# Latent and sparse prompt attention: outputs by query, divided by the softmax sum behind the value product

## The chip, the cores and the metric

The kernel runs on one core of one Trainium2 chip. The metric is the device time of one execution in microseconds. The median of three runs of the kernel before is 2569.67 us, the lowest 2569.64 and the highest 2575.63.

## What is computed

One step of a two-layer encoder for 512 prompt frames of a new stream and 64 sample frames of an old one with 1024 cached positions. Each layer runs a feed-forward block, then one projection whose columns feed four kinds of attention, then an output projection, then a second feed-forward block. The two kinds that the change touches end in the same softmax; cut to its core:

```python
def _softmax_attend(q, k, v, mask):                     # latent attention (MLA), 4 heads, value width 64
    s = jnp.einsum('bqhd,bkhd->bhqk', q, k).astype(jnp.float32) * (q.shape[-1] ** -0.5)
    p = jax.nn.softmax(jnp.where(mask[None, None], s, NEG_INF), axis=-1).astype(v.dtype)
    return jnp.einsum('bhqk,bkhd->bqhd', p, v)

def block(qp, qb, qib, wib):                            # sparse attention (DSA), 4 heads, one value of width 64
    ...
    _, idx = lax.top_k(score, n_sel)
    ...
    s = jnp.einsum('bqhd,bqkd->bhqk', qb, ks).astype(jnp.float32) * (DH_B ** -0.5)
    p = jax.nn.softmax(jnp.where(valid[:, None], s, NEG_INF), axis=-1).astype(vs.dtype)
    return jnp.einsum('bhqk,bqkd->bhqd', p, vs)
```

The other two kinds are stick-breaking attention and differential attention. Prompt queries are taken in four tiles of 128 (tile tt sees 128(tt+1) keys), the 64 sample queries form a fifth.

## The kernel before

A layer's mixing stage has two parts. In the first the projection's columns are computed piece by piece (matmuls of L629 to L631 into psG, a long supply of work for TensorE that depends on little), and beside them run MLA, the stick-breaking tiles, the top-k of the sparse attention's sample scores and of its prompt scores. In the second the differential and the sparse tiles run, with the rest of the prompt top-k, beside the output projection (L1095). The parts are generators that are merged by weights; the order of each engine's instructions is then fixed by a list scheduler when the program is built, from the order in which the code issues the work and from the buffers that it finds free. No wait or order is written by hand.

A prompt tile of MLA (L1157 to L1177) and of DSA (L1460 to L1485) handles two heads j at a time. `softmax_pair` (L698) puts the scores of each head into a psA bank, takes the negative row maximum on VectorE (L709), the exponential on ScalarE with the row sum (L710), and the reciprocals of both sums on VectorE (L712, tile rs). VectorE then multiplies each head's exponentials by its reciprocal (L1171 for MLA, L1479 for DSA). `pT_prompt` (L715) turns them with one transpose on TensorE for each block of 128 keys (L101) and copies the turned blocks out of psT, head 0 on VectorE (L87), head 1 on ScalarE (L85). `av_prompt` (L726, matmul in L730) multiplies with the values: the value block (128 keys x 64) is the stationary operand, the turned weights (128 x 128) are the moving one, head 0 fills rows 0 to 63 of the psO bank and head 1 rows 64 to 127. What stands in psO is the output by feature, which `put_o` copies into the operand of the output projection. Both kinds have 8 such calls in a layer, so there are 32 in the program. The stick-breaking and differential tiles use `pT_prompt` and `av_prompt` too, and they and the sample tiles use the same psO bank, of which there is one; psA, psT and psG have two banks each, psQ one.

Other lines that are named below: `scaled` (L97) is a ScalarE activation with a scale per row; a stick-breaking tile's weights are made by `stick_weights` with L1311, L1314, L1317 and L1318 on VectorE and L1312, L1313 and L1319 (the last step) on ScalarE; the prompt top-k repeats L977 (MAX) and L978 (MATCH_REPLACE) on VectorE 16 times for each of three query tiles; L1328 and L579 on VectorE rotate and split keys and queries; L1002 swaps rows on TensorE for the sample top-k; L1364 (VectorE) combines the two softmaxes of a differential tile, L760 is the exponential of a sample tile.

Of the kernel before, what the change touches and what calls it, by code (L numbers as in the profile page):

```python
# [13 lines left out]
ALU = mybir.AluOpType  # L14
# [22 lines left out]
class Builder:  # L37
# [17 lines left out]
    def t(self, pool, shape, dt=F32, tag="t"):  # L55
        return pool.tile(shape, dt, tag=tag, name=self.name(tag))
# [658 lines left out]
    def pT_prompt(self, P, i, k):  # L715

        ps = self.psT()
        for b in range(i + 1):
            self.transpose(ps[:, b * 128:b * 128 + 128], P[:, b * 128:b * 128 + 128])
        t = self.t(self.mp, [128, 512], tag="PT")  # L720
        n = (i + 1) * 128
# [3 lines left out]
    def av_prompt(self, PTs, V, i):  # L725
# [5 lines left out]
                                      start=(kt == 0), stop=(kt == i))  # L731
        return ps

    def put_o(self, o, c, t0, m, src, p0=0, p1=128):
        self.evac(self.turn(c), o[0][p0:p1, c, t0:t0 + m], src)

# [44 lines left out]

    def av_sample(self, out, PT, Vc, Vn):

        for j in range(8):
            self.nc.tensor.matmul(out, Vc(j), PT[:, j, :], start=(j == 0), stop=False)  # L785
        self.nc.tensor.matmul(out, Vn, PT[0:64, 8, :], start=False, stop=True)

# [96 lines left out]
    def ix_b(self, wi, kip, kis):  # L884
# [7 lines left out]
        for hb in range(2):  # L892
            for tt, m, ps, r in self.win(800 + 256 * hb, 256, tts=range(1, 5)):
# [3 lines left out]
                if tt < 4:  # L897
                    L = 128 * (tt + 1)
                    for j in range(4):
                        h = hb * 4 + j  # L900
                        pa = self.psA()
                        for k in range(2):
                            nc.tensor.matmul(pa[:, 0:L], qT[:, j * 128:j * 128 + 128], kip[:, k * 512:k * 512 + L],
                                             start=(k == 0), stop=(k == 1))
                        rl = t([128, 512], tag="PT")
                        nc.scalar.activation(rl[:, 0:L], pa[:, 0:L], AF.Relu)
# [196 lines left out]
    def mla(self, o):  # L1103
        nc, I, l = self.nc, self.i, self.l
# [3 lines left out]
        kT0, kT1, vp, lat = self.four(self.xp, "xT")  # L1108
# [43 lines left out]
        for tt, (t0, m) in enumerate(TT):  # L1152
            q = t([128, 4, 96], tag="q")
            nc.sync.dma_start(q[:m].rearrange("p h d -> p (h d)"), self.dq["a"][t0:t0 + m, :])
            ps = self.psQ()
            for h in range(4):
                self.transpose(ps[:96, h * m:h * m + m], q[:m, h, :])  # L1157
            qT = t([128, 512], tag="qT")
            self.scaled(qT[:96, 0:4 * m], ps[:96, 0:4 * m], scale)
            yield  # L1160
            if tt < 4:
                L = t0 + 128
                for pr in range(2):
                    def scores(j, out):
                        h = 2 * pr + j
                        nc.tensor.matmul(out, qT[:96, h * 128:h * 128 + 128], kT[pr][:96, j * 512:j * 512 + L],
                                         start=True, stop=True)
                    P, rs = self.softmax_pair(scores, L)
                    PT = []
                    for j in range(2):  # L1170
                        nc.vector.tensor_scalar(P[:, j, 0:L], P[:, j, 0:L], rs[:, j:j + 1], None, ALU.mult)  # L1171
                        PT.append(self.pT_prompt(P[:, j, :], tt, j))
                    po = self.av_prompt(PT, lambda kt, j: vp[:, kt * 256 + (2 * pr + j) * 64:
                                                             kt * 256 + (2 * pr + j) * 64 + 64], tt)
                    self.put_o(o, pr, t0, 128, po[:, 0:128])
                    yield
            else:  # L1177
                ps = self.psQ()
                for h in range(4):
                    nc.tensor.matmul(ps[:, h * 64:h * 64 + 64], wkT[:, h * 128:h * 128 + 128],  # L1180
                                     qT[0:64, h * 64:h * 64 + 64], start=True, stop=True)
                ql = t([128, 256], tag="ql")
                nc.scalar.copy(ql, ps[:, 0:256])
                ol = t([128, 256], tag="ql")
                for pr in range(2):
                    lq, lr = ql[:, pr * 128:pr * 128 + 128], qT[64:96, pr * 128:pr * 128 + 128]

                    def mms(out, s):
                        nc.tensor.matmul(out, lq, lats[:, s], start=True, stop=False)
                        nc.tensor.matmul(out, lr, krs[64:96, s], start=False, stop=True)  # L1190
                    P, rs = self.softmax_sample(self.sample_scores(mms))
                    nc.vector.tensor_scalar(P[:, 0:LS], P[:, 0:LS], rs, None, ALU.mult)
                    PT = self.pT_sample(P)
                    pol = self.psO()
                    self.av_sample(pol[:, 0:128], PT, lambda j: cr[j], mrow[4][0:64, 0:128])
                    nc.scalar.copy(ol[:, pr * 128:pr * 128 + 128], pol[:, 0:128])
                    yield
                po = self.psO()
                for h in range(4):
                    nc.tensor.matmul(po[64 * (h % 2):64 * (h % 2) + 64, (h // 2) * 64:(h // 2) * 64 + 64],  # L1200
                                     wkv[:, 1, h * 64:h * 64 + 64], ol[:, h * 64:h * 64 + 64], start=True, stop=True)
                for pr in range(2):
                    self.put_o(o, pr, 512, 64, po[:, pr * 64:pr * 64 + 64])
# [236 lines left out]
    def dsa(self, o, sel):  # L1440
        nc, I, O, l = self.nc, self.i, self.o, self.l
# [8 lines left out]
        kv = t([128, 4, 128], tag="kv")  # L1450
# [7 lines left out]
        for tt, (t0, m) in ((tt, TT[tt]) for tt in DSA_ORDER):  # L1458
# [3 lines left out]
            if tt < 4:  # L1462
                L = t0 + 128
# [5 lines left out]
                for pr in range(2):  # L1469
                    def scores(j, out):  # L1470
                        lhs = qT[:, (2 * pr + j) * 128:(2 * pr + j) * 128 + 128]
                        nc.tensor.matmul(out, lhs, kp[:, 0:L], start=True, stop=False)  # L1472
                        nc.tensor.matmul(out, lhs, kp[:, 512:512 + L], start=False, stop=(tt == 0))
                        if tt:
                            nc.tensor.matmul(out, self.identR, bias, start=False, stop=True)
                    P, rs = self.softmax_pair(scores, L, tt == 0, True)
                    PT = []
                    for j in range(2):
                        nc.vector.tensor_scalar(P[:, j, 0:L], P[:, j, 0:L], rs[:, j:j + 1], None, ALU.mult)  # L1479
                        PT.append(self.pT_prompt(P[:, j, :], tt, j))  # L1480
                    po = self.av_prompt(PT, lambda kt, j: kv[:, kt, 64:128], tt)
                    self.put_o(o, pr, t0, 128, po[:, 0:128])
                    yield
            else:
# [3 lines left out]
                for pr in range(2):  # L1488
# [12 lines left out]
                    P, rs = self.softmax_sample(self.sample_scores(mms), True)  # L1501
                    nc.vector.tensor_scalar(P[:, 0:LS], P[:, 0:LS], rs, None, ALU.mult)
                    PT = self.pT_sample(P, True)
                    po = self.psO()
# [32 lines left out]
    def run(self):  # L1537
        self.load_x()
        for l in range(DEPTH):
# [13 lines left out]
DSA_ORDER = (4, 0, 1, 2, 3)  # L1553
STICK_AT = (0, 1)
BUFS = dict(Pb=4, op=6, P=4, mrow=5, gq=4, gx=3, rt=3, qs=3, qT=2, PT=3, q=2, qm=1, mx=8, sm=6, rs=6, m1=3, s1=4, lr=4,
            ki=1, ql=2, m8=4)

_INS = ['x_prompt', 'x_sample', 'cache_mla', 'cache_dsa', 'cache_sb', 'cache_diff', 'norm_ff1', 'norm_mix', 'w_in',
        'mla_q_norm', 'mla_w_qb', 'mla_kv_norm', 'mla_w_kvb', 'diff_lambda', 'diff_norm', 'w_out', 'norm_ff2',
# [60 lines left out]
```

## Time and profile before

| | |
|---|---|
| median of the runs | 2569.67 us |
| the profiled execution | 2569.89 us |
| its span | 2568.1 us |
| TensorE (PE) busy | 2459.5 us, 96% |
| VectorE (DVE) busy | 1878.8 us, 73% |
| ScalarE (ACT) busy | 1251.2 us, 49% |

The span is the time from the first to the last instruction of the profiled execution; 1.8 us lie around it. In the trace the mixing stage of layer 0 lies at about 425 to 870 us and that of layer 1 at about 1690 to 2130 us; the rest is feed-forward. MLA's prompt tiles run between 565 and 620 and between 1815 and 1871 us, the stick-breaking prompt tiles up to 715 and 1982 us, DSA's prompt tiles at 770 to 870 and 2040 to 2127 us. A float32 matmul is two instructions in the trace, so L730 shows 640 instructions for its 320 matmuls. In the timeline a matmul's time overlaps the next one's; the distance between two starts is what it costs TensorE.

### The profile page before, as it was taken

How to read it: one execution, taken by the hardware profiler on the slowest of the kernel's cores; microseconds unless marked ns; L12 is line 12 of the kernel's file. 1: busy time of each engine (PE TensorE's matmuls, PEld its weight loads, DVE VectorE, ACT ScalarE, POOL GpSimd, SP SyncE). 2: the span in 40 equal slices, each digit the busy share in tenths (PEclk: the TensorE clock that was granted, in tenths of full speed). 3: DMA queues.
4: the chain of work that ended last, by engine and by line, in shares of the span. 5: the costliest groups of instructions: out<-in, count | busy, mean ns of one | idle time of the engine just before them, and what ended most of it. 6: DMA issues, size and time to landing. Idle time of an engine off the chain costs nothing. (4 is left out here: it accounts for less than half of the span.)

```text
span 2568.1 us, 44800 instructions
## 1 busy us (share of the span) xinstructions
PE 2459.5 (96%) x17275; PEld 2262.5 (88%) x17275; DVE 1878.8 (73%) x3866; ACT 1251.2 (49%) x2684; POOL 144.4 (6%) x255
## 2 busy tenths in 40 slices
PE   8999998999998899999999999989999988999998
PEld 7999998887775699999989999978877667999997
DVE  7858574798976696766697675648999676958574
ACT  5525253544555553544554353535445564625352
POOL 0000002200100100000100000022001001000001
PEclk9999998999999999999999999989999999999999
DMA  4313223243331123231423232233342312322222
GB/s 136 117 65 105 77 91 96 75 126 89 83 124 46 67 90 107 84 107 58 120 86 125 74 110 71 73 106 90 114 105 70 106 49 75 114 70 97 99 67 70
DMA packets 188581, 233.40 MB, mean 91 GB/s; under 512 B 79452, under 2 KB 143120, under 8 KB 188368
## 3 DMA queue, kind: packets, MB, share of 16 engines
q1 hardware_dynamic: 188368, 230.54, 28.9%
q8 instruction: 136, 2.23, 0.4%
q14 instruction: 77, 0.63, 0.1%
HBM read 211.76 MB, written 18.73 MB: 90 GB/s over the span
## 5 line engine op out<-in xcount | busy, mean ns | idle before, releaser
L563 PE MATMUL psA<-h,opd 128*128 128x288 f32 x3936 | 526.8, 296 | 0.0
L563 PEld LDWEIGHTS psA<-h,opd 128*128 128x128 f32 x3936 | 525.4, 189 | 0.0
L439 PE MATMUL psA<-T,opd 128*128 128x288 f32 x2880 | 396.2, 295 | 0.0
L439 PEld LDWEIGHTS psA<-T,opd 128*128 128x128 f32 x2880 | 387.2, 188 | 0.1
L439 PE MATMUL psA<-aH,opd 128*128 128x288 f32 x2240 | 366.6, 300 | 14.0 <-ACT aH L389 11.8
L439 PEld LDWEIGHTS psA<-aH,opd 128*128 128x128 f32 x2240 | 324.5, 191 | 17.0 <-ACT aH L389 14.2
L425 ACT CAST opd<-S 128x512 fp32r<-128x512 f32 x320 | 194.5, 621 | 160.6 <-PE psA L563 124.2
L426 DVE TENSOR_TENSOR opd<-S,opd 128x512 fp32r<-128x512 f32 x320 | 215.1, 688 | 75.9 <-ACT opd L425 72.4
L425 ACT CAST opd<-raw 128x512 fp32r<-128x512 f32 x272 | 163.8, 620 | 167.6 <-PE psA L563 82.2
L426 DVE TENSOR_TENSOR opd<-raw,opd 128x512 fp32r<-128x512 f32 x272 | 181.5, 687 | 66.1 <-ACT opd L425 66.0
L629 PE MATMUL psG<-whl,aH 128*128 128x256 f32 (+1 forms) x672 | 202.5, 302 | 15.7 <-ACT whl L299 15.3
L630 PE MATMUL psG<-whl,aH 128*128 128x256 f32 (+1 forms) x672 | 200.4, 298 | 0.8 <-DVE whl L300 0.7
L439 PE MATMUL psA<-aL,opd 128*128 128x288 f32 x1120 | 198.3, 300 | 0.0
L631 PE MATMUL psG<-whl,aL 128*128 128x256 f32 (+1 forms) x672 | 196.8, 293 | 0.0
L559 DVE TENSOR_TENSOR opd<-raw,opd 128x512 fp32r<-128x512 f32 (+1 forms) x176 | 114.1, 653 | 90.1 <-ACT opd L558 88.4
L558 ACT CAST opd<-raw 128x512 fp32r<-128x512 f32 (+1 forms) x176 | 103.5, 592 | 156.0 <-PE psA L563 120.4
L507 ACT COPY e<-psA 128x288 f32<-128x288 f32 x240 | 96.1, 400 | 159.8 <-PE psA L439 159.1
L568 DVE SCALAR_TENSOR_TENSOR xT<-psA,xT 128x288 f32<-128x288 f32 x192 | 79.5, 452 | 123.9 <-PE psA L563 123.6
L439 PEld LDWEIGHTS psA<-aL,opd 128*128 128x128 f32 x1120 | 168.4, 192 | 0.2
L1095 PE MATMUL psG<-op,whl 128*128 128x288 f32 x512 | 145.8, 412 | 2.2 <-DVE op L1397 1.0
L629 PEld LDWEIGHTS psG<-whl,aH 128*128 128x128 f32 x672 | 128.3, 191 | 20.7 <-ACT whl L299 15.7
L630 PEld LDWEIGHTS psG<-whl,aH 128*128 128x128 f32 x672 | 128.3, 191 | 8.3 <-issue 3.3
(428 smaller groups left out, 4073.2 us busy)
## 6 DMA issues: line engine op xcount, KB each, us to landing
raw<-in_wgu SPq DMA_DIRECT2D x176, 512.0 KB, 3.7
raw<-in_wdn SPq DMA_DIRECT2D x128, 256.0 KB, 3.0
raw<-in_w_in SPq DMA_DIRECT2D x36, 512.0 KB, 3.8
whl<-in_w_out SPq DMA_DIRECT2D x48, 256.0 KB, 3.9
raw<-in_wdn SPq DMA_DIRECT2D x48, 192.0 KB, 2.6
xs<-xT SPq DMA_DIRECT2D x16, 288.0 KB, 2.1
xT<-xs SPq DMA_DIRECT2D x8, 576.0 KB, 5.2
g<-in_wdn SPq DMA_DIRECT2D x16, 192.0 KB, 2.5
```

The source lines that it names most:

```text
L425: self.nc.scalar.copy(o[:, 0, :], x)
L426: self.nc.vector.tensor_tensor(o[:, 1, :], x, o[:, 0, :], ALU.subtract)
L439: self.nc.tensor.matmul(ps, o[:, w, c * 128:c * 128 + 128], a[:, c, :], start=start and i + c == 0, stop=stop and i == 2 and c == 3, skip_ ...
L507: nc.scalar.copy(t, ps)
L558: nc.scalar.copy(o[:, 0, 0:n * 128], r)
L559: nc.vector.tensor_tensor(o[:, 1, 0:n * 128], r, o[:, 0, 0:n * 128], ALU.subtract)
L563: nc.tensor.matmul(ps[h][:, 0:HALF], o[:, a, c * 128:c * 128 + 128], H[j][c][:, b, h * HALF:h * HALF + HALF], start=j + i + c == 0, stop=j ...
L568: nc.vector.scalar_tensor_tensor(xv, ps[h][:, 0:HALF], 0.5, xv, ALU.mult, ALU.add)
L629: nc.tensor.matmul(ps[:m, 0:n], a, hi, start=(c == 0), stop=False)
L630: nc.tensor.matmul(ps[:m, 0:n], a, lo, start=False, stop=False)
L631: nc.tensor.matmul(ps[:m, 0:n], b, hi, start=False, stop=(c == KC - 1))
L1095: nc.tensor.matmul(ps[k][:, 0:HALF], wt[:, sl], a[:, hs[k]], start=(c == 0), stop=(c == n - 1))
```

## The change

In the MLA and DSA prompt tiles the two multiplications by rs on VectorE are gone: the exponentials are turned as they are. A new function takes the place of `av_prompt` there. It makes the turned block (128 keys x 128 queries) the stationary operand and the value block (128 x 64) the moving one, so that a head's output comes by query, 128 rows of 64 columns, head 0 in columns 0 to 63 of the psO bank and head 1 in columns 64 to 127, one head after the other. Two ScalarE activations copy them to a new SBUF tile ot and multiply each row by its reciprocal. One transpose on TensorE turns ot into columns 128 to 255 of the same psO bank, and `put_o` copies it from there as before. The stick-breaking, differential and sample tiles are as they were.

```diff
+    def av_rows(self, PTs, V, i, rs):
+
+        ps = self.psO()
+        ot = self.t(self.mp, [128, 128], tag="ot")
+        for j in range(2):
+            out = ps[:, 64 * j:64 * j + 64]
+            for kt in range(i + 1):
+                self.nc.tensor.matmul(out, PTs[j][:, kt * 128:kt * 128 + 128], V(kt, j), start=(kt == 0), stop=(kt == i))
+        for j in range(2):
+            self.scaled(ot[:, 64 * j:64 * j + 64], ps[:, 64 * j:64 * j + 64], rs[:, j:j + 1])
+        self.transpose(ps[:, 128:256], ot)
+        return ps[:, 128:256]
...
                     P, rs = self.softmax_pair(scores, L)
-                    PT = []
-                    for j in range(2):
-                        nc.vector.tensor_scalar(P[:, j, 0:L], P[:, j, 0:L], rs[:, j:j + 1], None, ALU.mult)
-                        PT.append(self.pT_prompt(P[:, j, :], tt, j))
-                    po = self.av_prompt(PT, lambda kt, j: vp[:, kt * 256 + (2 * pr + j) * 64:
-                                                             kt * 256 + (2 * pr + j) * 64 + 64], tt)
+                    PT = [self.pT_prompt(P[:, j, :], tt, j) for j in range(2)]
+                    po = self.av_rows(PT, lambda kt, j: vp[:, kt * 256 + (2 * pr + j) * 64:
+                                                           kt * 256 + (2 * pr + j) * 64 + 64], tt, rs)
...
                     P, rs = self.softmax_pair(scores, L, tt == 0, True)
-                    PT = []
-                    for j in range(2):
-                        nc.vector.tensor_scalar(P[:, j, 0:L], P[:, j, 0:L], rs[:, j:j + 1], None, ALU.mult)
-                        PT.append(self.pT_prompt(P[:, j, :], tt, j))
-                    po = self.av_prompt(PT, lambda kt, j: kv[:, kt, 64:128], tt)
+                    PT = [self.pT_prompt(P[:, j, :], tt, j) for j in range(2)]
+                    po = self.av_rows(PT, lambda kt, j: kv[:, kt, 64:128], tt, rs)
...
-            ki=1, ql=2, m8=4)
+            ki=1, ql=2, m8=4, ot=2)
```

The new lines push the later ones down: in the changed kernel the new matmul is L741, L1166 is L1179, L1189 is L1199, L1311 is L1321, L1419 is L1429, L1095 is L1108, L977 and L978 are L990 and L991. The schedule changes with the new durations and buffers, all through the mixing stages.

On TensorE, an MLA tile with two key blocks in layer 0 (tt 1, the first pair of heads). A row is line, operation, output and inputs, and the size of the output; x2 stands for two alike in a row. Before:

```order
L629 MATMUL psG_7403<-whl_7398,aH_4315 128x256
L630 MATMUL psG_7403<-whl_7399,aH_4315 128x256
L631 MATMUL psG_7403<-whl_7398,aL_4316 128x256
L730 MATMUL psO_6577<-PT_6569,xT_6097 64x128
L730 MATMUL psO_6577<-PT_6575,xT_6097 64x128
L730 MATMUL psO_6577<-PT_6569,xT_6097 64x128
L730 MATMUL psO_6577<-PT_6575,xT_6097 64x128
L1166 MATMUL psA_6628<-xT_6097,qT_6624 128x384
```

After:

```order
L1179 MATMUL psA_6597<-xT_6097,qT_6551 128x256
L741 MATMUL psO_6579<-xT_6097,PT_6572 128x64 x2
L741 MATMUL psO_6579<-xT_6097,PT_6577 128x64 x2
L101 MATMUL psQ_6716<-ident,q_6714 96x128 x4
L630 MATMUL psG_7419<-whl_7415,aH_4315 128x256
L631 MATMUL psG_7419<-whl_7414,aL_4316 128x256
L101 MATMUL psO_6579<-ident,ot_6580 128x128
L629 MATMUL psG_7419<-whl_7414,aH_4315 128x256
```

The four matmuls that took the two heads by turns are now two of one head and two of the other, and six other matmuls stand between the last of them and the new transpose of ot, which needs ScalarE's two copies.

On TensorE, the first DSA tile of layer 0 (one key block). Before:

```order
L101 MATMUL psT_8752<-ident,Pb_8728 128x128
L730 MATMUL psO_8756<-PT_8749,kv_8272 64x128
L1419 MATMUL psA_8824<-aH_8161,qT_8795 128x256
L1095 MATMUL psG_9428<-op_6951,whl_9184 128x288
L730 MATMUL psO_8756<-PT_8754,kv_8272 64x128
L1419 MATMUL psA_8830<-aH_8161,qT_8795 128x256
```

After:

```order
L101 MATMUL psT_8766<-ident,Pb_8744 128x128
L741 MATMUL psO_8770<-kv_8288,PT_8764 128x64
L1429 MATMUL psA_8823<-aH_8177,qT_8813 128x256
L101 MATMUL psQ_9026<-ident,qs_9023 128x128 x2
L741 MATMUL psO_8770<-kv_8288,PT_8768 128x64
L1108 MATMUL psG_9454<-op_6107,whl_9208 128x288
L1108 MATMUL psG_9453<-op_6967,whl_9208 128x288
L101 MATMUL psO_8770<-ident,ot_8771 128x128
```

Here only two matmuls of the output projection stand between the last value product and the new transpose.

On VectorE, in layer 0, in a stick-breaking tile with three key blocks (L1311, in the changed kernel L1321, begins its weights P; S is the score tile of the prompt top-k). Before:

```order
L978 MATCH_REPLACE S_719_5149<-m_1674_9181,S_719_5149 128x512
L1311 TENSOR_SCALAR P_7215<-P_7214 128x2x384
L977 MAX m_1702_9269<-S_719_5149 128x8
L300 TENSOR_TENSOR whl_7947<-raw_7945,whl_7946 128x1024
L978 MATCH_REPLACE S_719_5149<-m_1702_9269,S_719_5149 128x512
L1314 TENSOR_TENSOR P_7215<-P_7214,P_7215 128x2x384
```

After:

```order
L991 MATCH_REPLACE S_719_5149<-m_1716_9299,S_719_5149 128x512
L1321 TENSOR_SCALAR P_7231<-P_7230 128x2x384
L990 MAX m_1717_9302<-S_719_5149 128x8
L991 MATCH_REPLACE S_719_5149<-m_1717_9302,S_719_5149 128x512
L990 MAX m_1761_9441<-S_719_5149 128x8
L991 MATCH_REPLACE S_719_5149<-m_1761_9441,S_719_5149 128x512
L1324 TENSOR_TENSOR P_7231<-P_7230,P_7231 128x2x384
```

One more step of the prompt top-k stands there, and the split of a weight (L300) has gone behind. Up to the last stick-breaking weights of a layer, VectorE's list holds three to four more MAX and three to four more MATCH_REPLACE of 128x512 than before.

## Rows read from the trace of the kernel before

**Rows 1.** The page: busy time by engine; the chain that ended last, by engine.

```profile
PE 2459.5 (96%) x17275; PEld 2262.5 (88%) x17275; DVE 1878.8 (73%) x3866; ACT 1251.2 (49%) x2684; POOL 144.4 (6%) x255
PE 21%; DVE 2%; ACT 1%; DMA 0%; issue 0%; SPq 0%; ACTq 0%; DVEq 0%
```

**Rows 2.** Busy time by stretch: stick-breaking of layer 1, DSA of both layers.

```profile
core 0: us, PE busy (x) PEld busy (x) DVE busy (x) ACT busy (x) POOL busy (x), PEclk, DMA share, GB/s
740.00:870.00 130.00, 120.63 (x680) 85.03 (x680) 92.31 (x282) 78.42 (x228) 4.99 (x6) 0.96 0.17 51
...
1910.00:1980.00 70.00, 63.13 (x434) 50.82 (x433) 67.76 (x117) 37.70 (x68) 9.07 (x14) 0.95 0.26 72
2010.00:2126.00 116.00, 107.06 (x627) 74.67 (x627) 84.55 (x265) 73.56 (x215) 3.37 (x4) 0.99 0.16 47
```

**Rows 3.** TensorE's timeline: start, time, line, operands; value products of one and three blocks.

```profile
566.60 0.28 PE L631 MATMUL psG<-whl,aL 128*128 128x256 f32 x1
566.71 0.28 PE L629 MATMUL psG<-whl,aH 128*128 128x256 f32 x1
566.93 0.44 PE L730 MATMUL psO<-PT,xT 128*64 128x128 f32 x4
567.29 0.39 PE L630 MATMUL psG<-whl,aH 128*128 128x256 f32 x1
...
598.14 0.88 PE L730 MATMUL psO<-PT,xT 128*64 128x128 f32 x12
598.95 0.39 PE L630 MATMUL psG<-whl,aH 128*128 128x256 f32 x1
```

**Rows 4.** Timelines of weight loads (one moving column each) and of TensorE (transposes).

```profile
423.78 0.52 PEld L287 LDWEIGHTS psQ<-ones,ssum 128*128 128x128 f32 x4 [1.75 <-DVE ssum L281]
...
2060.28 1.09 PE L101 MATMUL psT<-ident,P 128*128 128x128 f32 x8
2061.13 0.42 PE L1419 MATMUL psA<-aH,qT 128*128 128x384 f32 x1
```

**Rows 5.** VectorE's busy time in L1171 alone, then in L1479 alone, layer 0.

```profile
550.00:620.00 70.00, 5.50 (x16) 1.00 0.32 87
...
740.00:870.00 130.00, 5.41 (x16) 0.96 0.17 51
```

**Rows 6.** ScalarE groups of 128x64 in L97: busy, mean ns, idle before.

```profile
L97 ACT ACTIVATE gq<-psG,rtok 128x64 f32<-128x64 f32 x8 | 2.4, 311 | 5.0 <-DMA xT<-xs 4.4 <-DVE rt L579 0.5
...
L97 ACT ACTIVATE P<-psT 128x64 f32<-128x64 f32 x4 | 0.9, 224 | 0.4 <-PE psT L1270 0.4
```

**Rows 7.** ScalarE's timeline: the copy behind the value product at 598.14.

```profile
599.06 0.27 ACT L85 COPY op<-psO 128x128 f32<-128x128 f32 x1
```

**Rows 8.** TensorE's timeline: transposes of the last two stick-breaking tiles, layers 0 and 1.

```profile
704.92 1.97 PE L101 MATMUL psT<-ident,P 128*128 128x128 f32 x8 [3.00 <-ACT P L1319]
...
713.75 1.03 PE L101 MATMUL psT<-ident,P 128*128 128x128 f32 x8
...
1972.29 1.97 PE L101 MATMUL psT<-ident,P 128*128 128x128 f32 x8 [4.26 <-ACT P L1319]
...
1979.34 0.93 PE L101 MATMUL psT<-ident,P 128*128 128x128 f32 x7
```

**Rows 9.** ScalarE's timeline: the last step of the last stick-breaking tile, both layers.

```profile
712.22 1.06 ACT L1319 ACTIVATE P<-P 128x1024 f32<-128x1024 f32 x1 [2.22 <-DVE P L1318]
...
1978.16 1.07 ACT L1319 ACTIVATE P<-P 128x1024 f32<-128x1024 f32 x1
```

**Rows 10.** VectorE groups of the prompt top-k, 512 columns: busy, mean ns, idle.

```profile
L977 DVE MAX8 m<-S 128x8 f32<-128x512 f32 x32 | 21.9, 685 | 0.3
...
L978 DVE MATCH_REPLACE8 S<-m,S 128x512 f32<-128x512 f32 x32 | 21.6, 675 | 0.0
```

**Rows 11.** TensorE's waits at 740 to 870; the chain of waits at 2060.

```profile
PE psT L101 <- DVE P L1364: 3.0, 2, 1.9
...
2060.41 0.54 DVE Pb L1479 x2
```

## The prediction

> **What bounds the kernel now.** I read the busy times first, then the chain that ended last, then the busy time by stretch, and then the waits of the stretches in which changed lines run. TensorE is busy 96% of the span, VectorE 73%, and the chain that ended last is mostly TensorE [rows 1]: what lengthens TensorE's list lengthens the kernel, except where TensorE waits. It waits in two of the stretches. In the stick-breaking part of layer 1 (1910 to 1980) VectorE is busy 67.76 of 70 us and TensorE 63.13 [rows 2]: VectorE sets the end there. The last two tiles show it. In layer 0 TensorE idles 3.00 us for ScalarE's L1319, the last step of a tile's weights, and in layer 1 4.26 us; the eight transposes behind take 1.97 us against 1.03 at 713.75 [rows 8], so another 1 us is lost to the clock that fell in the wait. The last tile of each layer starts directly behind its own L1319, which ends at 712.22 + 1.06 = 713.28 and at 1978.16 + 1.07 = 1979.23 [rows 9], with the transposes at 713.75 and 1979.34 [rows 8]. In the DSA stretches TensorE idles 9 of 130 and 9 of 116 us, VectorE is at 71 and 73%, ScalarE at 60 and 63% [rows 2]: no engine is full, and the waits are for the chain of a softmax through all three.
>
> **TensorE's work.** Before, a value product of one key block runs from 566.93 to 567.29, one of three blocks from 598.14 to 598.95 [rows 3]: 0.81 - 0.36 = 0.45 for two blocks, so 0.22 a block (both heads side by side) and 0.14 over. It also starts 0.22 behind its predecessor where the row ahead has 0.11 [rows 3], 0.10 late. A layer has 8 calls with 20 blocks for each kind: 20 x 0.22 + 8 x 0.24 = 6.3 us. In DSA two calls a layer are cut in two by other matmuls, as in the order shown; each cut pays 0.36 + 0.10 once more, less its block: I take 7.2 us.
>
> After, a block is two instructions for each head, and each loads 128 columns of weights for only 64 moving ones. The row nearest to that is the group whose four loads serve one moving column each: four in 0.52 us, so at most 0.13 each; transposes with 128 moving columns go eight in 2061.13 - 2060.28 = 0.85, 0.106 each [rows 4]. With 1 and with 128 columns the step is the same, so the load sets it, and for 64 columns I take 0.11: 4 x 0.11 = 0.44 a block, 8.8 us for 20, and 8 transposes of ot at 0.106, 0.85. That is 9.65 us a layer and kind: 3.35 more in MLA, 2.45 more in DSA, **11.6 us over both layers**. The other end: were the step set by the moving columns, 0.106 x 64/128 = 0.053, a block would cost 0.21, the kind 4.2 + 0.85 = 5.1, and TensorE would save 1.2 and 2.1 a layer.
>
> **VectorE and ScalarE.** VectorE loses 16 instructions a layer in each kind, 5.50 and 5.41 us busy [rows 5], 21.8 us in all. No TensorE wait stands on L1171, so in MLA they were covered by the projection's matmuls. In DSA 0.54 us of L1479 stands on the chain once [rows 11]. ScalarE gains 64 copies of 128x64: 311 ns is the row with a scale per row, 224 the one without [rows 6]. I take 0.3, 0.61 a pair, 19.5 us in all (14.3 by the lower row). ScalarE has room for them, but they queue behind its exponentials.
>
> **The turn-around of ot.** A copy behind a value product now starts 599.06 - 598.95 = 0.11 after the next matmul [rows 3, 7]. The transpose of ot waits for the pair on ScalarE: some 0.2 from the last value product's start to its result, 0.61 for the pair, 0.1 and 0.1 to hand over, 1.0 us. What covers it is what the order puts between. In the MLA tile shown those are four transposes and two projection matmuls, 6 x 0.11 = 0.66: 0.3 short. Through the rest of MLA the order has six or more, mostly; I count 0.8 us a layer. In the DSA tile shown there are only two matmuls, and one later DSA tile has a single one; summed over the eight calls I come to 1.3 us a layer, if ScalarE takes the pair at once, none if the stall falls into a wait that is there anyway. The last DSA tile has its turn-around at the end of the layer's mixing, 0.5 us.
>
> **Where it lands: MLA and stick-breaking.** TensorE gets 3.35 + 0.8 = 4.15 us more per layer ahead of the last stick-breaking tiles, and has 4.0 us (3.00 and 1.0 of slow clock) to recover in layer 0, some 5.3 in layer 1 [rows 8]. But recovering takes that VectorE comes earlier, and the order fills most of its 5.4 us: three or four more MAX and MATCH_REPLACE at 685 and 675 ns, 5.0 us [rows 10], stand ahead of the last weights, for a few small splits and rotations that go behind, of which some filled gaps only. I take 1.5 us earlier for the last L1319 in each layer (0.3 to 2.6). Layer 0: the last transposes then start at 713.28 - 1.5 + 0.1 = 711.9, 1.8 earlier than before. TensorE is there in time: 713.75 - 4.0 + 4.15 = 713.9, less 35 projection matmuls (0.11 to 0.12 each, 4.1) and L1002 (0.4) that the new order leaves for behind, 709.4. These are still to be done: -1.8 + 4.5 = **+2.7**. Layer 1: 13 matmuls go behind, 1.5 us; TensorE would be there at 1979.34 - 5.3 + 4.15 - 1.5 = 1976.7, VectorE lets it go at 1977.8: -1.5 + 1.5 = **0**. Behind that both layers are TensorE's, and the rest of VectorE's saving (the top-k that is done early) buys nothing.
>
> **Where it lands: DSA.** TensorE +2.45, stalls 0.9 of the 1.3, the end 0.5; less 0.8 for L1479 on the chain (it is there 0.54 once, and some tiles wait less visibly), and less 0.6 because a part of the added 3.9 falls into the 7% and 8% in which TensorE idles and VectorE, relieved, hands over L1364 (3.0 us of waits [rows 11]) a little sooner: **+2.45 a layer**, between 0 and 4.3.
>
> **Sum.** 2.7 + 0 + 2 x 2.45 = +7.6 on the profiled 2569.89; that run is 0.2 over the median. I put it at **2577 us**, with 2570 to 2584 for this case by its terms' bounds. A measurement here can tell about 0.3%, 7.7 us, so the forecast lies at the edge of what can be told from no change.
>
> A page speaks to this too. The Trainium skill, "TensorEngine Tiling (Array Packing)", Key Properties, says that a change of tiling mode drains TensorE. The 0.10 and 0.14 us at the ends of a group with 64 output rows agree with that; with 128 rows they go, which the sum already has from the rows.
>
> **Rivals.**
> (a) *Nothing is given back.* TensorE's 11.6, the stalls of 2 x (0.8 + 1.3) and the ends 2 x 0.5 all lie on its path, and the waits for L1319 stay as they are because the top-k in front takes up VectorE's time: +16.8, 2586.5. For it: the order does put 5.0 us of top-k there. Against: 3 to 4 us of idle TensorE lie directly behind. It decides for slower from the point where more than half of the 16.8 stays. 0.13.
> (b) *ScalarE holds the single psO bank.* The pair and the transpose keep psO some 1.3 us longer, and L1319 or an exponential of 1.06 us [rows 9] ahead of the pair adds to it; the differential and sample tiles queue for the same bank. Half of 1.06 at each of 16 DSA tiles is +8.5, with the case's own +7.6 some 2585. For it: ScalarE's 60% in DSA [rows 2]; against: most uses of psO lie further apart. 0.07.
> (c) *VectorE was the bound.* Its saving comes off the chain: the waits of 4.0 and 5.3 us vanish (+0.2 and -1.2), and DSA, whose chain loses 5.4 us of VectorE's 92, gets 2.5 a layer back: -6, 2564, beyond the edge of faster if DSA gives 3.5. For it: VectorE at 97% in the stretch 1910 to 1980 [rows 2]. Against: the order refills it, and in DSA it is at 71%. 0.14, of which 0.08 faster.
> (d) *The moving columns set the step.* TensorE saves 2 x (1.2 + 2.1) = 6.6; with the waits that VectorE gives back (1.5 a layer) and half of the stalls, 2.1, it is -7.5, 2562. Against: the one-column group that takes as long as 128 columns [rows 4]. 0.05.
> The Trainium skill has this rule in "TensorE: Matmul & The Clock Gate", Back-to-back issue gap, for an isolated matmul: the gap goes with the number of moving columns. The trace disagrees by the group just named.
>
> **How the numbers follow.** The forecast's case has 0.61, of which 0.40 lies within 0.3% and 0.21 above. With (a) 0.13 and (b) 0.07 slower, (c) 0.08 faster and 0.06 within, (d) 0.05 faster: faster 0.13, same 0.46, slower 0.41. The range goes from (c), 2564, to 2588, just over (a) and (b); it leaves out the faster half of (c) with (d) and what goes wrong in more than one way.
>
> **What would show it.** Right: L741 steps of 0.11; the wait for the last stick-breaking tiles shorter by some 1.5 us a layer and moved to the very last tile; stretches 740 to 870 and 2010 to 2126 longer by 2 to 3 us; the transposes of ot waiting for L97 under 2 us a layer. Wrong: steps of 0.05, or waits of ot of 1 us at every tile, or DSA stretches that end sooner than before.

## The result

The changed kernel takes 2588.51 us in the median of five runs (2582.75 to 2594.87), beside 2571.12 us for the kernel before in the same five rounds (2569.64 to 2575.63). The ratio is 1.0063 with a 95% interval of 1.0047 to 1.0078: 0.63% slower, 16 us. The forecast was 2577 us, 7.3 us more than before. The profiled execution of the changed kernel took 2590.39 us, 20.5 us more than that of before, so its stretches add up to a little more than the medians differ.

The page of the changed kernel, busy time by engine, answers to [rows 1]:

```profile
PE 2473.9 (96%) x17307; PEld 2290.6 (88%) x17307; DVE 1860.8 (72%) x3802; ACT 1263.5 (49%) x2748; POOL 146.6 (6%) x255
```

VectorE is 18 us less busy, ScalarE 12 us more, TensorE 14 us more. Of the 20.5 us by which this execution is longer, 14 are TensorE's busy time, and the other 6 are time in which TensorE idles.

Where the time went is seen in the stretch from the first latent score to the last output-projection matmul of a layer. The first two rows are before, the other two after; the columns are the stretch, its length, the busy time of TensorE, its weight loads, VectorE, ScalarE and GpSimd, then TensorE's granted clock as a share of 2.4 GHz, and the DMA's share and rate. (MLA of layer 1 begins at 1826.70 us before, not at 1815.)

```profile
561.11:882.70 321.59, 305.43 (x1909) 229.83 (x1909) 257.77 (x653) 175.29 (x464) 25.93 (x42) 0.98 0.30 86
1826.70:2148.77 322.07, 304.42 (x1910) 228.83 (x1909) 257.03 (x654) 174.96 (x463) 26.09 (x42) 0.98 0.30 86
```

```profile
561.72:889.03 327.31, 307.96 (x1926) 238.85 (x1926) 248.20 (x621) 181.27 (x497) 27.41 (x42) 0.99 0.29 84
1834.62:2169.26 334.64, 315.25 (x1926) 247.21 (x1926) 249.06 (x622) 181.97 (x496) 26.44 (x42) 0.95 0.29 83
```

Layer 0 takes 5.7 us more, layer 1 takes 12.6 us more, though both have the same instructions, in orders that differ in places. Layer 1 also ran at a mean clock of 0.95 where before had 0.98, layer 0 at 0.99. Some 2 us more lie outside the two stretches, 0.6 ahead of the first and 1.6 between them.

The new value products, from TensorE's timeline of the changed kernel (start, time, line, operands):

```profile
598.10 0.78 PE L741 MATMUL psO<-xT,PT 128*128 128x64 f32 x6
598.72 0.39 PE L101 MATMUL psQ<-ident,kc 128*128 128x128 f32 x2
...
603.11 1.00 PE L741 MATMUL psO<-xT,PT 128*128 128x64 f32 x8
603.92 0.37 PE L631 MATMUL psG<-whl,aL 128*128 128x256 f32 x1
```

Six steps take 0.62 us, eight take 0.81: 0.10 each, for 64 moving columns. That is the step of [rows 4], where 128 columns of weights are loaded for one or for 128 moving columns; the moving columns do not set it. A block costs 0.41 us against 0.22 in [rows 3].

The transposes of ot and ScalarE's pairs, from the changed kernel's view of the tile ot:

```profile
L97 ACT ACTIVATE ot<-psO,rs x64: 304/308/317, 566.8 to 2148.6; 128x64 f32<-128x64 f32 x64
...
  PEld psO L101: 2.4, 7
...
  PE psO L101: 0.5, 2
```

A copy takes 308 ns in the median. In the whole program TensorE's matmuls waited for ot twice, 0.5 us together, and its weight loads, which run ahead of them, seven times, 2.4 us; so TensorE lost between 0.5 and some 3 us to it.

TensorE's waits in the latent and stick-breaking parts of the changed kernel, layer 0 and then layer 1 (us in total, times, the longest); the last two lines are the waits for L1319 before, in the same parts of both layers, and L1329 is what was L1319:

```profile
PE psG L629 <- DVE gx L623: 2.7, 1, 2.7
PE psT L101 <- ACT P L1329: 2.4, 2, 1.3
PE psG L629 <- DVE rt L579: 1.1, 1, 1.1
```

```profile
PE psT L101 <- ACT P L1329: 6.2, 3, 3.4
PE psG L629 <- DVE rt L579: 0.6, 1, 0.6
```

```profile
PE psT L101 <- ACT P L1319: 3.9, 2, 3.0
...
PE psT L101 <- ACT P L1319: 5.3, 2, 4.3
```

And where they stand in the timeline, beside [rows 8]: layer 0, then layer 1.

```profile
705.07 0.39 PE L629 MATMUL psG<-whl,aH 128*128 128x256 f32 x1 [2.72 <-DVE gx L623]
713.02 1.09 PE L101 MATMUL psT<-ident,P 128*128 128x128 f32 x8 [1.11 <-ACT P L1329]
...
1981.65 1.09 PE L101 MATMUL psT<-ident,P 128*128 128x128 f32 x8 [2.00 <-ACT P L1329]
1987.98 1.97 PE L101 MATMUL psT<-ident,P 128*128 128x128 f32 x8 [3.42 <-ACT P L1329]
```

Of the last two tiles of a layer, TensorE waited before at one, the last but one, 3.00 and 4.26 us. After, it waits twice: in layer 1 at both tiles, in layer 0 at the last one and, ahead of the last but one, under another name. There TensorE's next projection matmul needs a psG bank that VectorE's L623 has yet to read. L623 could have read it from 701.31 on, when ScalarE's L622 had ended, but it stands behind steps of the stick-breaking weights in VectorE's list:

```profile
700.64 2.33 DVE L1327 TENSOR_TENSOR_SCAN P<-zero,P 128x512 f32<-128x512 f32 x2
...
703.48 1.22 DVE L1328 TENSOR_TENSOR P<-P,P 128x1024 f32<-128x1024 f32 x1
704.61 0.41 DVE L623 TENSOR_TENSOR gx<-gx,psG 64x256 f32<-64x256 f32 x1
```

Counted from the first latent score of the layer, which is 0.6 us later than before in layer 0 and 7.9 in layer 1, the transposes of the last tile come 1.3 us earlier in layer 0 (713.02 against 713.75) and 0.7 us later in layer 1 (1987.98 against 1979.34).

### The profile page after: what moved, and what is told of

Its sections match the earlier page's. It is cut to its first block, busy times and chain, and to the rows that moved or that the text cites. A ratio compares the mean times of both kernels' runs of the same rounds, so it can differ in the third digit from the quotient of the medians.

```text
span 2588.6 us, 44915 instructions
## 1 busy us (share of the span) xinstructions
PE 2473.9 (96%) x17307; PEld 2290.6 (88%) x17307; DVE 1860.8 (72%) x3802; ACT 1263.5 (49%) x2748; POOL 146.6 (6%) x255
## 4 chain that ended last, share of the span: by engine, by line
PE 62%; DVE 5%; ACT 3%; DMA 1%; issue 1%; POOL 0%; SPq 0%; ACTq 0%; DVEq 0%; POOLq 0%
PE psA L439 23%; PE psA L563 16%; PE psG L1108 4%; PE psT L439 4%; PE psT L101 2%; PE psG L630 1%; PE psG L629 1%; PE psQ L101 1%; PE psG L631 1%; PE psO L741 1%; PE psO L798 1%; PE psO L730 1%; DVE opd L426 0%; DMA kv<-out_dsa_p 0%; PE psA L1383 0%
## 5 line engine op out<-in xcount | busy, mean ns | idle before, releaser
L1108 PE MATMUL psG<-op,whl 128*128 128x288 f32 x512 | 147.5, 417 | 0.5 <-ACT gq L97 0.4
```

Source lines behind the costliest of these rows:

```text
L1108: nc.tensor.matmul(ps[k][:, 0:HALF], wt[:, sl], a[:, hs[k]], start=(c == 0), stop=(c == n - 1))
```

## Experiments

Theory A was that TensorE's added work lies on its path and VectorE's relief is used up by top-k steps; theory B, the prediction's, that the relief comes back in part and the sparse tiles lose the rest; theory C that ScalarE's pair stands in the chains; theory D that the waits for L1319 are the chain between VectorE and ScalarE by itself. Theory E was formed from what these runs showed. All ratios are to the kernel before in the same rounds, with 95% intervals; 0.1% is 2.6 us. Each run is one draw of the order by the list scheduler, and the last part of this section finds that such draws of the same work lie 4 to 17 us above the kernel before; a difference between two runs that is not larger than that shows the work's own worth only where a trace bears it out.

### One kind alone

In `mla_only` the sparse tiles are as before, in `dsa_only` the latent tiles.

```diff
 mla_only, in the sparse tiles
-                    PT = [self.pT_prompt(P[:, j, :], tt, j) for j in range(2)]
-                    po = self.av_rows(PT, lambda kt, j: kv[:, kt, 64:128], tt, rs)
+                    PT = []
+                    for j in range(2):
+                        nc.vector.tensor_scalar(P[:, j, 0:L], P[:, j, 0:L], rs[:, j:j + 1], None, ALU.mult)
+                        PT.append(self.pT_prompt(P[:, j, :], tt, j))
+                    po = self.av_prompt(PT, lambda kt, j: kv[:, kt, 64:128], tt)
```

> Only the latent tiles get the new form, the sparse tiles stay as before. Theory A (TensorE's added work stays on its path, VectorE's relief is used up): the trace of the changed kernel is 4.2 us behind at the last projection matmul of layer 0 and another 4.2 us behind at that of layer 1, so 2571.1 + 8 = 2579 us. Theory B (VectorE's relief comes back as in the prediction, 2.7 us in layer 0 and 0 in layer 1, and the rest of the loss is in the sparse tiles): 2574 us.

Measured 1.0044 (1.0029 to 1.0059): +11.3 us.

> Only the sparse tiles get the new form. Theory A: about half of the loss, +6 to +9 us, 2577 to 2580. Theory B: most of it, +12 to +14 us, 2583 to 2585, because ScalarE's pair stands in the chain of the differential and sparse softmaxes. The prediction's own sum had +4.9.

Measured 1.0011 (1.0001 to 1.0020): +2.8 us.

The sum, 14, is that of the full change within the intervals. By these two runs the loss sits with the latent tiles, where theory B and the prediction had put the least, though their difference is within the scatter of draws; theory B's numbers for both are out. Theory A's holds for the latent tiles within the interval and is too high for the sparse ones: TensorE's added work is about the same in the two kinds (3.1 and 3.3 us a layer, below), and the sparse tiles lost less than it while the latent ones lost more.

### VectorE's relief alone, and the new form without it

`no_scale` drops the multiplications and puts nothing in their place; `rows_mul` has the new form and the multiplications.

```diff
 no_scale, both kinds
-                    PT = []
-                    for j in range(2):
-                        nc.vector.tensor_scalar(P[:, j, 0:L], P[:, j, 0:L], rs[:, j:j + 1], None, ALU.mult)
-                        PT.append(self.pT_prompt(P[:, j, :], tt, j))
+                    PT = [self.pT_prompt(P[:, j, :], tt, j) for j in range(2)]
```

> The kernel before without the two multiplications on VectorE and nothing put in their place (the division by the softmax sum is left out in the latent and sparse prompt tiles). It measures what VectorE's relief is worth by itself. Theory A: within 2 us of before, because top-k steps take the time. Theory B: 4 to 8 us faster (1.5 us earlier at each last stick-breaking tile, 0.8 us and more of the sparse tiles' chain in each layer).

Measured 1.0001 (0.9990 to 1.0012): nothing, with 22 us less on VectorE.

> The new value product, ScalarE's two copies (with the constant 1) and the transpose of ot, but VectorE multiplies the exponentials as before. It measures the new form without the relief. Theory A: as the changed kernel, 2586 to 2590. Theory B: 5 to 8 us slower than the changed kernel, 2592 to 2597.

Measured 1.0079 (1.0063 to 1.0095): +20 us, 4 us over the changed kernel, with intervals that overlap: between the marks of A and B. (With the constant its copies take 222 ns in place of 308.)

The waits of `no_scale` in the latent and stick-breaking parts, layer 0 and layer 1 (L1316 is what was L1319):

```profile
PE psT L101 <- ACT P L1316: 3.3, 2, 2.8
...
PE psT L101 <- ACT P L1316: 5.1, 2, 4.2
```

They are those of [rows 8], 3.00 and 4.26 us, nearly unchanged: 2.8 and 4.2 us at the longest. Taking VectorE's work away does not bring the last stick-breaking weights earlier: counted from the first latent score, the last L1316 ends 1.4 us later in layer 0 and 2.7 in layer 1 than L1319 before. VectorE's time was filled with other steps, as the 70 us up to the last weights of layer 1 show, beside 67.76 in [rows 2] (fourth number: VectorE's busy time):

```profile
1910.84:1980.84 70.00, 63.31 (x439) 51.09 (x438) 68.30 (x114) 39.13 (x71) 9.00 (x14) 0.96 0.32 80
```

Theory B's mechanism fails in this trace; that the time is unchanged is the result of one draw.

### Work on TensorE alone

```diff
 mla_twice, against the kernel before
-    def av_prompt(self, PTs, V, i):
+    def av_prompt(self, PTs, V, i, n=1):
...
-        for kt in range(i + 1):
+        for kt in list(range(i + 1)) * n:
...
-                                                             kt * 256 + (2 * pr + j) * 64 + 64], tt)
+                                                             kt * 256 + (2 * pr + j) * 64 + 64], tt, 2)
```

> The kernel before with each value product of the latent prompt tiles run twice, the second run from the start again (the result is the same). It puts only work on TensorE ahead of the stick-breaking tiles: 20 blocks of 0.22 us a layer, 4.4 us, 8.8 in all, with VectorE and ScalarE as before. Theory A (TensorE's work there stays on the path, although TensorE waits 3 to 4 us at the last stick-breaking tiles behind it): +7 to +11 us. Theory B (TensorE's idle time at the last stick-breaking tiles takes it in): +0 to +3 us.

Measured 1.0064 (1.0051 to 1.0077): +16.5 us. That is more than the work put in, 8.8 us, so neither theory gives it. The two layers, in the view of the stretches above:

```profile
561.58:886.60 325.02, 307.70 (x1987) 232.29 (x1985) 257.50 (x653) 174.38 (x463) 25.75 (x42) 0.98 0.30 85
1833.35:2168.61 335.26, 314.95 (x1987) 239.45 (x1985) 258.91 (x654) 175.38 (x462) 27.83 (x42) 0.96 0.29 82
```

Layer 0 lengthens by 3.4 us, layer 1 by 13.2, from the same 4.4 us of work in each. TensorE's idle time did not take the work in: its waits for L1319 are 4.7 and 5.9 us here, 3.9 and 5.3 before. Layer 1 also shows a granted clock of 0.96.

### The copies on VectorE

```diff
 ot_dve, against the changed kernel
-            self.scaled(ot[:, 64 * j:64 * j + 64], ps[:, 64 * j:64 * j + 64], rs[:, j:j + 1])
+            self.nc.vector.tensor_scalar(ot[:, 64 * j:64 * j + 64], ps[:, 64 * j:64 * j + 64], rs[:, j:j + 1], None, ALU.mult)
```

> The changed kernel with the two scaled copies of ot on VectorE in place of ScalarE. Theory A (TensorE's work and the order make the loss): as the changed kernel, within 4 us. Theory C (ScalarE's pair stands in the chains, rival (b) of the prediction): 5 us or more faster than the changed kernel.

Measured 1.0083 (1.0067 to 1.0098): +21 us, 5 us over the changed kernel with intervals that overlap, so just past theory A's 4 us and not on theory C's side. The waits of the changed kernel agree, and bear on rival (b). In its whole trace TensorE waits for a copy that frees psO only here:

```profile
PE psO L741 <- DVE op L87: 1.0, 2, 0.5
```

Its weight loads wait for such copies 4.0 us in all, 2.4 before. That, and the 0.5 to 3 us for ot, is all that the trace shows of ScalarE's pairs and the longer hold of psO on TensorE; rival (b) had put 8.5 us on it. Theory C falls.

### Without the prompt top-k

```diff
 nt_before against the kernel before, nt_after against the changed kernel
-            for _ in range(16):
-                m8 = self.t(self.mp, [128, 8], tag="m8")
-                nc.vector.max(m8, S[i])
-                nc.vector.match_replace(S[i], m8, S[i], SENT)
-                yield
+            yield
```

> The kernel before without the steps of the prompt top-k (L977 and L978 are left out, so the sparse tiles select nothing), some 50 us less of VectorE per layer. If the top-k steps in front of the stick-breaking weights hold TensorE up (theory A's reason why VectorE's relief buys nothing), the waits for L1319 shrink from 9.2 us to under 3 and the kernel is 5 us or more faster. If those waits are the softplus chain between VectorE and ScalarE itself (theory D), they stay at 6 us or more.

Measured 1.0042 (1.0028 to 1.0056): +10.8 us, slower, although 96 pairs of steps are gone from VectorE. TensorE's waits in the latent and stick-breaking part, layer 0 and then layer 1, and in the sparse part of layer 0 (L1315 was L1319, L1360 was L1364):

```profile
PE psT L101 <- ACT P L1315: 2.5, 3, 1.9
PE psG L630 <- DVE whl L300: 1.8, 2, 1.3
```

```profile
PE psG L629 <- DVE rt L579: 2.9, 2, 1.6
PE psT L101 <- ACT P L1315: 1.5, 3, 0.9
```

```profile
PE psT L101 <- DVE P L1360: 5.0, 3, 2.0
PE psQ L101 <- ACT qbdd L1403: 3.3, 1, 3.3
```

The waits for stick-breaking weights, 7.3 us in [rows 8] alone and 9.2 with the small ones of other tiles, shrink to 4.0, between the marks of A and D: the top-k steps make about half of them. The last tile's transposes then come 4 us sooner in layer 0, 709.60 against 713.75. But its last projection matmul comes 6.2 later, 725.36 against 719.14, and other waits come up (L300, L579). The stretch of layer 0 from the first latent score to the last projection matmul, before and then without the top-k:

```profile
561.11:719.42 158.31, 153.40 (x1086) 122.08 (x1086) 146.51 (x328) 82.24 (x190) 13.36 (x26) 0.99 0.32 87
```

```profile
566.90:725.64 158.74, 152.07 (x1065) 120.69 (x1065) 114.14 (x236) 81.39 (x188) 18.33 (x28) 0.99 0.36 97
```

This part is not where the kernel loses. The profiled execution is 14.8 us longer. Of that, 5.8 lie ahead of the first latent score of layer 0 and 4.8 between the two layers' stretches; the part shown is 0.4 longer in layer 0 and 5.6 shorter in layer 1; the sparse parts, where L1364 costs 5.0 us in place of 3.0, are 4.4 and 6.0 longer; 1.1 fewer lie at the end. The edit also takes 15 of 16 yields a tile from its generator, so the merge itself is another. It is no clean measure of VectorE's work, but it shows that a kernel with less VectorE work can be slower.

> The changed kernel without the steps of the prompt top-k, against nt_before. Theory A (loss by TensorE's own work, which lies on its path, and by top-k steps in the way): the difference to nt_before is TensorE's work alone, +10 to +14 us. Theory D: the difference is as between the two kernels with top-k, +14 to +18 us.

Measured 1.0080 (1.0063 to 1.0098), 0.38% over `nt_before`: 9.8 us, give or take 6. That is on theory A's side of the mark, near TensorE's added work, but the interval reaches the other.

### The same work, another order

The odd results have one thing in common: each edit makes the list scheduler draw the order of the mixing stages anew. Theory E is that the order of the kernel before is a good draw for its durations. Three edits of the kernel before change no work on any engine:

```diff
 heads_swapped
-            for j in range(2):
+            for j in (1, 0):
                 self.nc.tensor.matmul(ps[64 * j:64 * j + 64, 0:128], V(kt, j), PTs[j][:, kt * 128:kt * 128 + 128],
 evac_swapped, in the latent tiles
-                        PT.append(self.pT_prompt(P[:, j, :], tt, j))
+                        PT.append(self.pT_prompt(P[:, j, :], tt, 1 - j))
 mla_early; after_mla_early is the same edit of the changed kernel
-("mla", 0.2)
+("mla", 0.25)
```

> The kernel before with the two heads of every value product in L730 taken in the other order: same instructions, same work on every engine, but the schedule is drawn anew (352 of TensorE's 16342 matmuls and 146 of VectorE's 3710 instructions stand in another place of their order). Theory E (the order of the kernel before is a good draw for its durations, and an edit that makes the scheduler draw again loses some 3 to 6 us a layer, whatever the edit does): +5 to +12 us. Theory A (only work counts, the order hardly): within 3 us of before.

Measured 1.0015 (1.0003 to 1.0026): +3.9 us.

> The kernel before with the copies of the turned weights in the latent prompt tiles the other way round (head 0 on ScalarE, head 1 on VectorE): same work on every engine, the order drawn anew (380 matmuls and 257 VectorE instructions elsewhere). Theory E: +5 to +12 us. Theory A: within 3 us.

Measured 1.0066 (1.0053 to 1.0079): +17 us, as much as the change itself.

> The kernel before with the weight of the latent tiles in the merge with the projection at 0.25 in place of 0.2: same instructions, issued a little earlier (525 matmuls and 306 VectorE instructions elsewhere, more than without the multiplications). Theory E: +5 to +12 us. Theory A: within 3 us.

Measured 1.0035 (1.0022 to 1.0047): +9.0 us.

> The changed kernel with the same weight at 0.25: its work, another draw of its order (555 matmuls elsewhere). Theory E: the draws of the changed kernel scatter by several us, so this one may lie from 2576 to 2592; by TensorE's measured work alone (12.8 us over both layers, with waits as before) it would be 2584. Theory A: as the changed kernel within 3 us, 2586 to 2591.

Measured 1.0061 (1.0049 to 1.0073): +15.7 us, as the changed kernel.

The stretches of `evac_swapped`, same columns as above:

```profile
561.36:894.16 332.80, 312.93 (x1909) 234.50 (x1909) 257.99 (x652) 174.66 (x464) 26.78 (x42) 0.96 0.29 83
1841.24:2169.88 328.64, 308.69 (x1909) 232.74 (x1909) 257.69 (x653) 175.18 (x463) 24.74 (x42) 0.97 0.30 84
```

In this execution TensorE has the same 1909 matmuls as before and is busy 7.5 us longer with them in layer 0, at a granted clock of 0.96. VectorE and ScalarE are busy as before. The waits of its sparse part in layer 0 answer to [rows 11]:

```profile
PE psT L101 <- DVE P L1364: 5.0, 3, 2.0
PE psA L1472 <- ACT P L760: 3.3, 2, 1.8
```

L1364 costs 5.0 us where it was 3.0, and the wait for L760 comes twice. So the loss has two parts here: waits, and a lower clock. The clock is not the order's alone: 23 executions of the kernel before on one chip, all in one order, have mean granted clocks of 0.978 to 0.985 and times of 2582.0 to 2567.5 us. Over all executions `evac_swapped` has 0.9795 in the mean of six where the kernel before has 0.9828 in the 17 beside them, so there the lower clock goes with the order; `mla_early`, with +9.0 us, has 0.9828 too, and loses without it. That the order hardly counts falls: two of the three edits that change no work are far beyond 3 us, the third is at that mark with its interval on both sides. Theory E's size fits one of them, one lost less and one more; the scatter is 4 to 17 us.

## Why the prediction came out as it did

**Forecast and cause.** The prediction gave 0.46 to no change and 0.41 to slower by over 0.3%, which it was; its central number was 9 us short. The time is that of rival (a), 2586.5 us; its mechanism, nothing is given back, holds for the waits: those for L1319 (now L1329) and L623 are 5.1 us in layer 0 and 6.2 in layer 1, against 3.9 and 5.3 for L1319 before. That its sum fits is in part luck: much of the stalls in it did not come, and what came in their place, longer waits, a lower clock in layer 1 and perhaps a worse draw of the order, is not in it.

**TensorE's work: right, a little short.** The term was 11.6 us. By the distances between starts in the trace, summed over all calls, the latent calls cost 8.3 us of L741 and 0.9 of transposes a layer, the sparse ones 8.7 and 1.6. Before, it was 6.1, with the 0.5 us by which the groups start late, and 7.0 (without; the sparse groups start late by as much after as before). That is 3.1 and 3.3 more a layer, 12.8 in all. The steps of 0.10 (0.11 forecast) were smaller. Most of the sparse transposes cost 0.11, as forecast, but in each layer two cost 0.35 and 0.56, because what follows them waits. Rival (d), by which the moving columns set the step, falls.

**The turn-around of ot: wrong by its size.** The time from the start of the last L741 to the transpose was about right: where nothing else holds the transpose up, it starts 0.89 us behind (14 of the 32 calls), for 1.0. But the sum carried 3.4 us of stalls, and TensorE's matmuls waited 0.5 us for ot, some 3 at most. Half a dozen matmuls in between cover it but for 0.1 us; only where a single one stands there, in one DSA tile of each layer, did TensorE idle, 0.25 us each.

**ScalarE: right.** 308 ns a copy for 311, and hardly a cost on the path; rival (b) falls with `ot_dve` and the waits for psO beside it.

**VectorE's relief: the step that failed.** The prediction took 1.5 us earlier for the last weights of each layer. Counted from the first latent score, in layer 0 the last L1329 ends 0.9 us earlier than L1319 did; the stretch from that score to the last projection matmul then is 3.7 us longer, 2.7 forecast. In layer 1 it ends 0.8 later, and the stretch is 4.7 longer where the forecast was 0. The forecast there had the waits shrink and with them the microsecond of slow clock; instead TensorE waits 3.42 us at the very last tile, and the eight transposes behind take 1.97 us, at the lower level of 1.2 GHz, where [rows 8] has 0.93 for the seven on record. That the wait would move to the last tile was forecast rightly; that it would be shorter was not. The reading behind the 1.5 was that VectorE, 97% busy, was short of time there. Much of that was top-k steps that the scheduler puts into gaps: in `no_scale` VectorE is as busy with the multiplications gone, and the last weights come no sooner; in `nt_before`, without the top-k, it is busy 72% of the latent and stick-breaking part of layer 0 (93% before), and that part is 0.4 us longer. Rival (c), VectorE was the bound, is not borne out: its gain came with neither run. In layer 1 of `nt_before`, though, that part is 5.6 us shorter; how much of this is VectorE's and how much the other merge's stays open.

**The sparse tiles: open.** +2.45 a layer was forecast. Alone (`dsa_only`) they cost 2.8 us for both layers, 1.4 a layer, in one draw. In the trace of the full change layer 0 has 2.0, from its last projection matmul to its last output-projection matmul; layer 1 has 7.8. Much of the difference lies around 2100 to 2120 us of the changed kernel, here with the columns of the stretches above:

```profile
2100.00:2120.00 20.00, 15.36 (x78) 11.96 (x77) 11.69 (x31) 11.35 (x29) 0.00 (x0) 0.74 0.00 1
...
2108.49 1.97 PE L101 MATMUL psT<-ident,P 128*128 128x128 f32 x8 [1.91 <-DVE P L1374]
2110.25 1.49 PE L1399 MATMUL psQ<-P,bones 128*128 128x384 f32 x2
```

The wait of 1.91 us is an old one, L1364 of [rows 11]; from the eight transposes behind it to the next start are 1.76 us where [rows 4] has 0.85, which is the lower of the two clock levels, 1.2 GHz in place of 2.4. The mean granted clock over these 20 us is 0.74. Before, the same wait stands in both layers, and there it is layer 0 whose transposes are slow behind it, 1.77 us, and layer 1 whose are not, 0.92:

```profile
822.26 1.97 PE L101 MATMUL psT<-ident,P 128*128 128x128 f32 x8 [1.91 <-DVE P L1364]
824.03 1.49 PE L1389 MATMUL psQ<-P,bones 128*128 128x384 f32 x2
...
2089.38 1.09 PE L101 MATMUL psT<-ident,P 128*128 128x128 f32 x8 [1.91 <-DVE P L1364]
2090.30 1.14 PE L1389 MATMUL psQ<-P,bones 128*128 128x384 f32 x2
```

After, layer 0 goes fast behind it (0.93 from 828.98). So the clock makes layer 0's 2.0 too small and layer 1's 7.8 too large for what the change does there; that 2.0 is near the forecast is luck, and the mean is 4.9 a layer, twice the forecast and far above the 1.4 of `dsa_only`. The forecast had no term for the clock behind waits that stay.

**What it left out.** The prediction priced each moved instruction where a wait stood in its way, but took the rest of the order for neutral. The four draws of the old work lie at 0, 0.15, 0.35 and 0.66%, 0.29% in the mean; the two of the new work at 0.63 and 0.61%. From the means the change itself costs 0.33%, some 8.5 us, an estimate from six draws: less than TensorE's 12.8 us of work. The four draws alone spread over 0.66%, so this estimate does not secure the size, nor quite the sign. The rest of the 16 us, about half, would be the lost draw. How the 16 us of this one change divide between TensorE's work, waits, clock and draw is not settled by that: no run has the new work in the old order, which the scheduler cannot be given. `mla_early` and `after_mla_early` share a setting, and differ by 0.26%, 6.7 us.

## What to carry to other kernels

Where a scheduler draws the order, a kernel whose order is a good draw can lose some tenths of a per cent by an edit that changes no work, so an edit's own worth must be compared over several draws of both versions (swap two heads, change a merge weight), and a gain that is smaller than their scatter is not shown. A VectorE at 97% need not be the bound where a list scheduler has filled its gaps; take work off it and look in the trace whether the end comes sooner. The granted clock moves from one execution to the next, so what one trace shows of it is held against the clocks of all runs. And a value product with 64 output features is dearer by query than by feature: with 128 columns of weights for 64 moving ones a step took 0.10 us and a block 0.41, while two heads side by side had taken 0.22.

## What was not expected of the hardware

In single traces, the same 1909 matmuls of a layer's stretch kept TensorE busy between 304.4 and 312.9 us, as the granted clock's mean went from 0.98 to 0.96: in layer 0 of `evac_swapped` 7.5 of the 11.2 us lost are busy time at a lower mean clock. The same wait of 1.91 us was followed by eight transposes in 0.92 us in one layer and in 1.77 in the other, in one execution of one kernel. And 23 executions of the kernel before, all in one order, lay between 2567.5 us, at a mean clock of 0.985, and 2582.0, at 0.978. Doubling 4.4 us of matmuls came with 3.4 us more in one layer and 13.2 in the other, at clocks of 0.98 and 0.96.
